# Four sixths of each layer's modulation: from matmuls in the linear attention to ACT products and POOL sums during the RWKV scan

## The chip, the cores and the metric

The kernel runs on one core of one Trainium2 chip. The metric is the device time of one execution in microseconds (us), as the median of several runs. The engines are TensorE (PE in the rows, with its weight loads as PEld), VectorE (DVE), ScalarE (ACT), GpSimd (POOL) and SyncE (SP), which here issues nearly all DMA transfers. Each engine carries out its instructions in the order in which they stand in its own list, and waits at an instruction until what it needs is there.

## What is computed

Two layers of a token mixer and a feed-forward net work on 1024 latent tokens and 256 context tokens, width 1024, in fp32. All inputs of the mixer come from one projection (`w_in`); three mixers (retention, gated linear attention, RWKV) run on their parts of it. Each layer's norms are modulated by six vectors of 1024 numbers, once for the latent tokens and once for the context:

```python
mod_l = jax.nn.silu(c) @ w_mod[l] + b_mod[l]          # w_mod[l]: 1024 x 6144
mod_c = jax.nn.silu(c_ctx) @ w_mod[l] + b_mod[l]
sh1, sc1, gt1, sh2, sc2, gt2 = jnp.split(mod_l[:, None, :], 6, axis=-1)
...
u_lat = (_modulate(_rmsnorm(x, norm_mix_pre[l]), sh1, sc1) @ w_in[l]).astype(jnp.float32)
...
x = x + gt1 * _rmsnorm(y_lat, norm_mix_post[l])
f_lat = _swiglu(_modulate(_rmsnorm(x, norm_ffn_pre[l]), sh2, sc2), w_ffn_gate[l], w_ffn_up[l], w_ffn_down[l])
x = x + gt2 * _rmsnorm(f_lat, norm_ffn_post[l])
```

The change concerns the product of the two vectors with `w_mod`. Its first two parts (`sh1`, `sc1`) are wanted at the start of a layer, the other four (parts 2 to 5) only after the mixers.

## The kernel before

A layer runs in stages. First comes the RWKV preparation, then the scan: 20 calls of `next(rw)` (index k), each one step over chunks of 64 tokens in both directions. A step is a chain of small matmuls (ra, rd, rs), ACT copies (R, BKT, Ot) and VectorE updates (Sp). Its inputs come from DRAM by SP in tiles X (one buffer), SAV and XE. The chunk matrices behind it are inverted on POOL in five blocks of four chunks (lines 731 to 736), written out and read again as XE.

Beside the scan TensorE works on *dense tiles*: the projection's columns for the linear attention (`gla_in`) and for retention (`ret_in`). One dense tile is 24 matmuls, eight slices by three products of high and low parts (whi, wlo, xh, xl), into a PSUM bank `pd`. There are three such banks, handed out in program order (`pd()`, line 198). The result goes through a tile `st` to DRAM. `gla_back` (line 1809), a part of the linear attention's backward sweep, also uses pd banks.

What the scan's 20 steps do not reach of the dense tiles follows in the tail: `rwkv_out` (transposes `pn<-ident,fo`, POOL's fo and fy), the rest of `ret_in`, and the first calls of `ret`, whose matmuls write `rr`. Then the pools of the scan are closed, and the linear attention (`gla`, matmuls into `pg`) runs in PA = 7 calls together with the rest of retention. The modulation runs there: `mods(1)` in each call takes one part from the list `todo`, which is parts 2 to 5 of this layer, and in layer 0 also parts 0 and 1 of layer 1. One part in `mod` is sixteen loads of 256 KB (`wmod`, four buffers), 32 fp32 matmuls with the two vectors as weights (2 columns) and 256 columns of `w_mod` moving (64 records in the trace), four ACT copies, two transposes and two VectorE adds.

A scheduler sets each engine's order from the program's order, priorities and its own planning of times; the `high_priority` blocks bring `rt` and `ro` forward in the tail.

Of the kernel before, what the change touches and what calls it, by code (L numbers as in the profile page):

```python
# [10 lines left out]
AF = mybir.ActivationFunctionType  # L11
ALU = mybir.AluOpType
# [5 lines left out]
KT = 8  # L18
# [59 lines left out]
def blk_of(i):  # L78
    if i < 2:
        return 0, 128 * i  # L80
    if i < 6:
        return 1, 128 * (i - 2)
    return 2, 128 * (i - 6)
# [88 lines left out]
class Kern:  # L172
# [133 lines left out]
    def mod(self, l, V, p, parts, bufs):  # L306

        nc, I = self.nc, self.I
        if l not in self.modT:
            self.modT[l] = self.t(self.G, [128, 48, 2], f"modT{l}")  # L310
        mt = self.modT[l]
        for m in parts:
            ps = self.pn()
            for kt in range(KT):
                for hf in range(2):
                    w = self.t(p, [128, 512], "wmod", bufs=bufs)
                    self.dma(w, I["w_mod"][l, 128 * kt:128 * kt + 128, 1024 * m + 512 * hf:1024 * m + 512 * hf + 512])
                    for g in range(2):
                        q = 2 * hf + g
                        self.mm(ps[32 * q:32 * q + 2, 0:256], self.sc[:, kt, :], w[:, 256 * g:256 * g + 256],  # L320
                                start=(kt == 0), stop=(kt == KT - 1))
            row = self.t(p, [128, 256], "mrow", bufs=1)
            nc.vector.memset(row, 0.0)
            for g in range(4):
                nc.scalar.copy(row[32 * g:32 * g + 2, :], ps[32 * g:32 * g + 2, 0:256])
            pt = self.pn()
            for q in range(2):
                nc.tensor.transpose(pt[:, 128 * q:128 * q + 128], row[:, 128 * q:128 * q + 128], self.ident)
            bm = V["b_mod"][:, 8 * m:8 * m + 8].rearrange("p (g q) -> p g q", q=2)
            for s in range(2):  # L330
                nc.vector.tensor_tensor(
                    mt[:, 8 * m:8 * m + 8, s].rearrange("p (g q) -> p g q", q=2),
                    pt[:, 0:256].rearrange("p (q g r) -> p g q r", g=4, r=32)[:, :, :, s], bm, op=ALU.add)

    def mod_gain(self, l, V, part_scale, gname, add_one):

# [414 lines left out]
    def gla_in(self, l, W1, xh, xl, ctx_out):  # L751
        nc, I = self.nc, self.I
        w_in = I["w_in"][l]

        def qk(t0):
            c = GLA0 + (0 if t0 < 2 else 192)
            wh, wl = self.weights(W1, [(64 * h, w_in[:, c + 48 * h:c + 48 * h + 48]) for h in range(4)], 256)
            for t in (t0, t0 + 1):
                for b in range(3):
                    if b == 0 and t < 2 and not ctx_out:  # L760
                        continue
                    n0, n = BLK[b]
                    ps = self.pd()
                    self.dense_cm(ps[:, :n], wh, wl, xh[b], xl[b], 128 * (t % 2))
                    for o in range(0, n, 256):
                        st = self.t(self.st, [128, 256], "st", bufs=6)
                        if t < 2:
                            self.act(st, ps[:, o:o + 256], AF.Copy, scale=48.0 ** -0.5)
                        else:
                            nc.scalar.copy(st, ps[:, o:o + 256])  # L770
                        self.dma(self.QK[l][:, t, n0 + o:n0 + o + 256], st)
                    yield n / 100

        def vg(m):
            wh, wl = self.weights(W1, [(0, w_in[:, GLA0 + 384 + 256 * m:GLA0 + 640 + 256 * m])], 256)
            for i in range(10):
                b, o = blk_of(i)
                if i < 2 and m == 2 and not ctx_out:
                    continue
                ps = self.pd()  # L780
                self.dense_tm(ps[:, :256], wh, wl, xh[b][:, :, o:o + 128], xl[b][:, :, o:o + 128])
                st = self.t(self.st, [128, 256], "st", bufs=6)
                v = 256 if m == 0 else (128 if m == 1 else 0)
                self.evac(st, ps[:, :256])
                if v < 256:
                    self.silu(self.st, st[:, v:], st[:, v:])
                self.dma(self.VG[l][128 * i:128 * i + 128, 256 * m:256 * m + 256], st)
                yield 2.56

        yield from qk(2)  # L790
        yield from vg(0)
        yield from vg(1)
        yield 0
        yield from qk(0)
        yield from vg(2)

    def ret_in(self, l, W1, xh, xl, ctx_out):
        nc, I = self.nc, self.I
        w_in = I["w_in"][l]
        for m in (1, 2, 0, 3):  # L800
            wh, wl = self.weights(W1, [(0, w_in[:, 256 * m:256 * m + 256])], 256)
            for i in range(10):
                b, o = blk_of(i)
                if i < 2 and m in (0, 3) and not ctx_out:
                    continue
                ps = self.pd()
                self.dense_tm(ps[:, :256], wh, wl, xh[b][:, :, o:o + 128], xl[b][:, :, o:o + 128])
                st = self.t(self.st, [128, 256], "st", bufs=6)
                self.evac(st, ps[:, :256])
                if m == 3:  # L810
                    self.silu(self.st, st, st)
                self.dma(self.UR[l][128 * i:128 * i + 128, 256 * m:256 * m + 256], st)
                yield 2.56
# [952 lines left out]
    def run(self):  # L1766
# [7 lines left out]
        f = self.f_tiles(F, range(3))  # L1774
# [12 lines left out]
        for l in range(DEPTH):  # L1787
            V = self.V[l]
            ctx_out = l < DEPTH - 1
# [6 lines left out]
            rw = self.rwkv(l, V, ctx_out)  # L1796
# [10 lines left out]
            gi = self.gla_in(l, W1, xh, xl, ctx_out)  # L1807
            ri = self.ret_in(l, W1, xh, xl, ctx_out)
            gb = self.gla_back(l, gbk)
            for k in range(20):  # L1810
                next(rw)
                if k < N1:
                    run(gi, 77 / N1)
                if k == N1 - 1:
                    for c in gi:
                        if GA and c == 0:
                            break
                if N1 <= k < N2:
                    run(chain(gi, ri), DT / (N2 - N1))
                    run(gb, GR)  # L1820
            for _ in rw:
                pass
            self.grw.__exit__(None, None, None)
            gpsr.__exit__(None, None, None)
            self.banks = (0, 0, 1)
# [2 lines left out]
            gX, X = self.pool("X", side=self.o)  # L1828
            rt = self.ret(l, ctx_out, X)
            ro = self.rwkv_out(l, V, ctx_out, pf)  # L1830
            todo = [(l, m) for m in (2, 3, 4, 5)] + ([(1, 0), (1, 1)] if ctx_out else [])

            def mods(k):
                while k and todo:
# [49 lines left out]
            f = self.f_tiles(self.F01, bs)  # L1884
# [83 lines left out]
```

## Time and profile before

| | |
|---|---|
| median of 3 runs | 4197.41 us (4195.5 to 4204.27) |
| profiled execution, its own time | 4200.48 us |
| its span, first to last instruction | 4198.7 us |
| mean granted clock of TensorE | 0.951 of full speed |
| busy in the span: TensorE, VectorE, ACT, POOL | 3837.7 (91%), 2668.9 (64%), 1740.9 (41%), 1678.4 (40%) us |

Busy times are unions of intervals by engine. Matmuls are pipelined: one that follows another at 0.12 us may have a duration of 0.28. In layer 0 the scan lies from about 366 to 755 us of the span, the tail to 896, the linear attention to 1105; in layer 1 the scan ends at about 2950, the tail at 3055 and the linear attention at 3190.

### The profile page before, as it was taken

The page shows a single profiled execution, that of the slowest core. Times are in us where ns is not written, and L with a number is a line of the kernel's source. Part 1 is how long each engine was busy: PE and PEld are TensorE (multiplying, and loading weights), DVE is VectorE, ACT ScalarE, POOL GpSimd, SP SyncE. Part 2 cuts the span into 40 slices and gives each one's busy share as a digit, 9 for nine tenths or more (in the row PEclk, how much of TensorE's full clock was granted, in tenths as well). Part 3 has the DMA queues.
Part 4 walks back from the last instruction along what each step waited for, and adds up shares of the span by engine and source line. Part 5 has one row for each costly group of instructions (what it writes and reads, how often), then busy time and mean ns, then how long its engine had stood idle before and what let it go on. Part 6 is the DMA issues. An engine that isn't in the chain of part 4 may idle for free. (4 is left out here: it accounts for less than half of the span.)

```text
span 4198.7 us, 78278 instructions
## 1 busy us (share of the span) xinstructions
PE 3837.7 (91%) x30414; PEld 3170.7 (76%) x30414; DVE 2668.9 (64%) x4510; ACT 1740.9 (41%) x3490; POOL 1678.4 (40%) x1775
## 2 busy tenths in 40 slices
PE   6998999789988899999997997999889887999998
PEld 3777887776667888887785676888856667999876
DVE  3465657667647766665765464667667578556665
ACT  4443334244435644433423443343244355344432
POOL 3146630333338832224533245740433454222453
PEclk8998999999999899999998997999989889999999
DMA  5587545666433422225331387655673132212542
GB/s 174 137 229 192 142 130 151 186 188 192 141 122 126 151 103 80 81 90 192 132 106 55 86 232 198 137 140 141 206 225 117 57 126 89 86 71 95 185 163 95
DMA packets 624771, 582.55 MB, mean 139 GB/s; under 512 B 315276, under 2 KB 517264, under 8 KB 607504
## 3 DMA queue, kind: packets, MB, share of 16 engines
q1 hardware_dynamic: 624112, 576.50, 45.0%
q8 instruction: 240, 3.93, 0.4%
q0 software_dynamic: 288, 1.05, 0.1%
q14 instruction: 131, 1.07, 0.1%
HBM read 431.14 MB, written 146.28 MB: 138 GB/s over the span
## 5 line engine op out<-in xcount | busy, mean ns | idle before, releaser
L1464 POOL TENSOR_TENSOR slo<-raw,shi 128x512 fp32r<-128x512 f32 x467 | 690.9, 1494 | 964.6 <-ACT shi L1463 894.0
L1463 ACT CAST shi<-raw 128x512 fp32r<-128x512 f32 x478 | 293.0, 619 | 492.7 <-PE pd L246 196.3
L1741 DVE TENSOR_TENSOR f<-pm,f 128x512 f32<-128x512 f32 (+1 forms) x400 | 252.1, 635 | 186.7 <-PE pm L246 184.5
L246 PE MATMUL pm<-hh,shi 128*128 128x512 f32 (+1 forms) x880 | 333.8, 380 | 19.5 <-DVE f L1741 10.2
L246 PE MATMUL pm<-hl,shi 128*128 128x512 f32 (+1 forms) x880 | 327.2, 372 | 0.0
L246 PE MATMUL pm<-hh,slo 128*128 128x512 f32 (+1 forms) x880 | 326.3, 371 | 0.0
L447 POOL TENSOR_TENSOR wlo<-wraw,whi 128x512 fp32r<-128x512 f32 x120 | 166.8, 1399 | 386.7 <-ACT whi L446 376.1
L246 PE MATMUL pd<-whi,xh 128*128 128x256 f32 x1072 | 315.6, 296 | 1.9 <-DVE st L451 1.9
L246 PE MATMUL pd<-wlo,xh 128*128 128x256 f32 x1072 | 314.5, 294 | 1.8 <-POOL wlo L447 1.8
L246 PE MATMUL pd<-whi,xl 128*128 128x256 f32 x1072 | 315.0, 294 | 0.0
L246 PE MATMUL pd<-xl,whi 128*128 128x512 f32 (+1 forms) x720 | 278.1, 387 | 12.5 <-POOL xl L390 8.6
L246 PE MATMUL pd<-xh,whi 128*128 128x512 f32 (+1 forms) x720 | 276.9, 385 | 11.6 <-DVE xh L388 11.5
L246 PE MATMUL pd<-xh,wlo 128*128 128x512 f32 (+1 forms) x720 | 271.5, 377 | 1.1 <-POOL wlo L447 1.1
L1463 ACT CAST shi<-tw 128x512 fp32r<-128x512 f32 x200 | 123.6, 619 | 305.3 <-PE pd L246 231.9
L246 PEld LDWEIGHTS pd<-wlo,xh 128*128 128x128 f32 x1072 | 211.5, 197 | 10.3 <-issue 6.0
L246 PEld LDWEIGHTS pd<-whi,xh 128*128 128x128 f32 x1072 | 210.9, 197 | 9.2 <-DVE st L451 2.5
L246 PEld LDWEIGHTS pd<-whi,xl 128*128 128x128 f32 x1072 | 211.2, 197 | 5.8 <-issue 3.7
L246 PEld LDWEIGHTS pm<-hh,shi 128*128 128x128 f32 x880 | 167.5, 191 | 58.0 <-DVE f L1741 18.3
L246 PEld LDWEIGHTS pm<-hl,shi 128*128 128x128 f32 x880 | 167.8, 191 | 29.6 <-issue 1.7
L246 PEld LDWEIGHTS pm<-hh,slo 128*128 128x128 f32 x880 | 167.2, 190 | 28.9
L1464 DVE TENSOR_TENSOR slo<-tw,shi 128x512 fp32r<-128x512 f32 x200 | 145.1, 727 | 67.0 <-ACT shi L1463 66.7
L246 PEld LDWEIGHTS pd<-xl,whi 128*128 128x128 f32 x720 | 141.5, 197 | 53.3 <-POOL xl L390 13.5
(395 smaller groups left out, 11218.4 us busy)
## 6 DMA issues: line engine op xcount, KB each, us to landing
raw<-in_wgu SPq DMA_DIRECT2D x72, 1024.0 KB
wmod<-in_w_mod SPq DMA_DIRECT2D x192, 256.0 KB
raw<-in_wd SPq DMA_DIRECT2D x44, 1024.0 KB
wraw<-in_w_in SPq DMA_DIRECT2D x100, 256.0 KB
a<-ops SPq DMA_DIRECT2D x80, 288.0 KB
h<-h SPq DMA_DIRECT2D x44, 512.0 KB
h<-u SPq DMA_DIRECT2D x19, 1024.0 KB
X<-ops SPq DMA_DIRECT2D x36, 480.0 KB
```

The source lines that it names most:

```text
L246: return self.nc.tensor.matmul(out, l, r, start=start, stop=stop, skip_group_check=skip)
L447: nc.gpsimd.tensor_tensor(wl[i][:, :, w], r, wh[i][:, :, w].bitcast(F32), op=ALU.subtract)
L1463: self.nc.scalar.copy(hi, src)
L1464: e.tensor_tensor(lo, src, hi.bitcast(F32), op=ALU.subtract)
L1741: nc.vector.tensor_tensor(facc[b][:, m, :], ps, facc[b][:, m, :], op=ALU.add)
```

## The change

`mod_wide` computes parts 2 to 5 in half parts of 512 columns. For each of the eight slices of 128 rows it loads 128x512 of `w_mod`; ACT multiplies it by the vector's number of each partition (a Copy with a scale per partition), once for each of the two vectors, and POOL adds the product to the sum `macc`. The first slice goes straight into the sum. After eight slices eight fp32 matmuls with a column of ones (weights: 128 columns of macc) add over the partitions into a pd bank, and two VectorE adds bring in the bias. The buffers are: wmod two, mprod one, macc one. The second product is written over the loaded slice. Four slices are called for behind each scan step from k = 2 on (`N1` to `N2`), the rest behind the scan's last step and ahead of the closing of its pools. The list in the linear attention keeps only parts 0 and 1 of layer 1. The buffers of `st` in `gla_in` and `ret_in` go from six to four.

```diff
+    def mod_wide(self, l, V, p, parts):
...
+        for m in parts:
+            for hf in range(2):
+                acc = self.t(p, [128, 2, 512], "macc")
+                for kt in range(KT):
+                    w = self.t(p, [128, 512], "wmod", bufs=2)
+                    c = 1024 * m + 512 * hf
+                    self.dma(w, I["w_mod"][l, 128 * kt:128 * kt + 128, c:c + 512])
+                    v = (w, self.t(p, [128, 512], "mprod")) if kt else None
+                    for s in (1, 0):
+                        self.act(acc[:, s] if kt == 0 else v[s], w, AF.Copy, scale=self.sc[:, kt, s:s + 1])
+                        if kt:
+                            nc.gpsimd.tensor_tensor(acc[:, s], acc[:, s], v[s], op=ALU.add)
+                    yield
+                ps = self.pd()
+                for s in range(2):
+                    for j in range(4):
+                        self.mm(ps[:, 4 * s + j:4 * s + j + 1], acc[:, s, 128 * j:128 * j + 128], self.ones[:, 0:1])
+                o = 8 * m + 4 * hf
+                for s in range(2):
+                    nc.vector.tensor_tensor(mt[:, o:o + 4, s], ps[:, 4 * s:4 * s + 4], V["b_mod"][:, o:o + 4], op=ALU.add)
...
-                        st = self.t(self.st, [128, 256], "st", bufs=6)
+                        st = self.t(self.st, [128, 256], "st", bufs=4)
...
+            gmw, pmw = self.pool("pmw", side=self.a)
+            mw = self.mod_wide(l, V, pmw, (2, 3, 4, 5))
             for k in range(20):
                 next(rw)
...
                 if N1 <= k < N2:
                     run(chain(gi, ri), DT / (N2 - N1))
                     run(gb, GR)
-            for _ in rw:
-                pass
+                for _ in range(4):
+                    next(mw, None)
+            for g in (rw, mw):
+                for _ in g:
+                    pass
+            gmw.__exit__(None, None, None)
...
-            todo = [(l, m) for m in (2, 3, 4, 5)] + ([(1, 0), (1, 1)] if ctx_out else [])
+            todo = [(1, 0), (1, 1)] if ctx_out else []
```

In the order of instructions the change shows at two places. The first is TensorE in the tail of layer 0: dense matmuls (whi, wlo with xh, xl into pd) and the transposes of the RWKV output (ident with fo). Before, around one of these transposes:

```order
L246 MATMUL pd_8869<-whi_1319_7998,xh_108_313 128x256
L246 MATMUL pd_8869<-wlo_1321_8000,xh_108_313 128x256
L246 MATMUL pd_8869<-whi_1319_7998,xl_109_314 128x256
L1425 MATMUL pn_9756<-ident_67,fo_9743 128x128 x3
L246 MATMUL pd_8869<-whi_1319_7998,xh_108_313 128x256
L246 MATMUL pd_8869<-wlo_1321_8000,xh_108_313 128x256
```

Now, at the sixth of the eight half parts:

```order
L246 MATMUL pd_8399<-whi_1421_8380,xl_107_312 128x256
L1452 MATMUL pn_10280<-ident_67,fo_10267 128x128 x3
L1452 MATMUL pn_10389<-ident_67,fo_10376 128x128 x3
L246 MATMUL pd_8427<-ones_69,macc_7891 128x1 x8
L246 MATMUL pd_8649<-whi_1420_8379,xh_106_311 128x256
L246 MATMUL pd_8649<-wlo_1422_8381,xh_106_311 128x256
L246 MATMUL pd_8649<-whi_1420_8379,xl_107_312 128x256
L1452 MATMUL pn_10498<-ident_67,fo_10485 128x128 x3
```

The eight matmuls on macc stand between two dense tiles, and the dense matmuls of the next tile and the next transpose come behind them.

The second place is SP in the scan of layer 0, which issues the loads of a step: XE and SAV of the scan's chunk, X of a later one, and for the linear attention glr, gk, ur. Before:

```order
L249 DMA glr_6228<-lrg_16_85 16x128 x2
L249 DMA ur_22_91<-st_5967 128x256
L249 DMA XE_8358<-af_36_105 128x6x32
L249 DMA XE_8358<-xe_46_115 128x6x96
L249 DMA gk_6232<-qk_18_87 128x2x128
L249 DMA SAV_8355<-vt_49_118 64x384 x2
```

Now:

```order
L249 DMA wmod_5586<-in_w_mod 128x512
L249 DMA wmod_5851<-in_w_mod 128x512
L249 DMA wmod_5858<-in_w_mod 128x512
L249 DMA XE_8564<-af_35_104 128x6x32
L249 DMA XE_8564<-xe_45_114 128x6x96
L249 DMA gk_6096<-qk_18_87 128x2x128
L249 DMA wmod_5865<-in_w_mod 128x512
L249 DMA ur_22_91<-st_5803 128x256
L249 DMA SAV_8561<-vt_49_118 64x384 x2
```

The loads of `w_mod`, each of which needs one of two buffers to be free, stand ahead of and between the loads of the scan step.

## Rows read from the trace of the kernel before

**Rows 1.** Stretches A:B: length, busy us (count) by engine, clock, DMA share, GB/s.
```profile
366.00:620.00 254.00, 241.12 (x3412) 211.76 (x3412) 154.49 (x340) 93.09 (x268) 140.21 (x232) 0.97 0.56 142
620.00:750.00 130.00, 124.47 (x2128) 104.93 (x2127) 90.32 (x225) 53.32 (x155) 6.71 (x12) 1.00 0.49 138
750.00:890.00 140.00, 115.78 (x998) 109.42 (x998) 78.91 (x204) 33.73 (x81) 47.11 (x52) 0.94 0.61 179
896.00:1105.00 209.00, 192.30 (x1696) 127.48 (x1690) 163.42 (x378) 95.76 (x241) 82.80 (x85) 0.97 0.63 198
...
2945.00:3055.00 110.00, 95.65 (x814) 91.18 (x816) 67.78 (x181) 24.34 (x58) 46.41 (x59) 0.95 0.70 207
3055.00:3190.00 135.00, 120.05 (x989) 76.72 (x981) 93.09 (x223) 54.52 (x140) 41.34 (x45) 0.89 0.66 209
```

The engines stand in the order PE, PEld, DVE, ACT, POOL.

**Rows 2.** Stretches, instructions that touch wmod alone: PE busy, PEld busy.
```profile
905.00:1105.00 200.00, 39.04 (x368) 8.19 (x368) 0.99 0.62 197
3050.00:3182.00 132.00, 30.38 (x256) 5.23 (x256) 0.88 0.69 217
```

**Rows 3.** TensorE's waits, 905 to 1110 us: us in total, times, longest.
```profile
PE pn L246 <- DMA wmod<-in_w_mod: 6.6, 6, 1.5
```

**Rows 4.** Groups of POOL and ACT by shape: count | busy us, mean ns | idle before.
```profile
L447 POOL TENSOR_TENSOR wlo<-wraw,whi 128x512 fp32r<-128x512 f32 x20 | 26.0, 1309 | 91.7 <-ACT whi L446 91.7
...
L372 POOL TENSOR_TENSOR nacc<-nacc,nsq 128x512 f32<-128x512 f32 x33 | 49.9, 1511 | 33.8 <-ACT nsq L239 31.6 <-PE pm L246 2.2
...
L239 ACT ACTIVATE nsq<-f 128x512 f32<-128x512 f32 x81 | 51.0, 629 | 67.8 <-DVE nacc L370 40.6 <-POOL nacc L372 15.6 <-DVE f L412 6.6
```

The first is of 366 to 760 us, the others of the whole span.

**Rows 5.** TensorE in time, retention's products: start us, us, instruction, count.
```profile
986.11 0.39 PE L246 MATMUL rr<-Sl,qx 128*128 128x64 f32 x2
986.33 0.39 PE L246 MATMUL rr<-v,sc 128*128 128x64 f32 x2
```

**Rows 6.** SP and TensorE in time: a wmod load and the matmul it releases.
```profile
970.91 0.33 SPq L249 DMA_DIRECT2D wmod<-in_w_mod  x1
...
974.50 0.60 PE L246 MATMUL pn<-wmod,silc 128*2 128x256 f32 x4 [0.60 <-DMA wmod<-in_w_mod]
```

**Rows 7.** ACT in time: the scan's copy R in steps 13, 15, 19; layer 1, 18.
```profile
653.60 0.46 ACT L1341 COPY R<-ra 128x384 f32<-128x384 f32 x1
...
688.83 0.47 ACT L1341 COPY R<-ra 128x384 f32<-128x384 f32 x1
...
749.98 0.48 ACT L1341 COPY R<-ra 128x384 f32<-128x384 f32 x1 [1.55 <-PE ra L246]
...
2926.15 0.48 ACT L1341 COPY R<-ra 128x384 f32<-128x384 f32 x1 [1.32 <-PE ra L246]
```

**Rows 8.** TensorE in time, the tail of layer 0, and layer 1's last dense matmul.
```profile
775.40 1.21 PE L246 MATMUL pd<-guout,gz 128*128 128x130 f32 x4 [9.29 <-DVE gz L1006]
...
780.96 0.41 PE L246 MATMUL pd<-whi,xl 128*128 128x256 f32 x1
781.17 0.41 PE L246 MATMUL pd<-whi,xh 128*128 128x256 f32 x1
...
889.99 0.28 PE L246 MATMUL pd<-wlo,xh 128*128 128x256 f32 x1
890.11 0.28 PE L246 MATMUL pd<-whi,xl 128*128 128x256 f32 x1
...
3054.02 0.28 PE L246 MATMUL pd<-whi,xl 128*128 128x256 f32 x1
```

**Rows 9.** POOL and SP in time: an inverse written out, the later read of its block.
```profile
390.79 1.90 POOL L736 COPY LT<-L 96x1024 f32<-96x1024 f32 x1
...
431.45 1.80 SPq L249 DMA_DIRECT2D XE<-xe  x1
```

**Rows 10.** VectorE's update Sp, groups of 400 to 500 us and of 610 to 750.
```profile
L1353 DVE TENSOR_TENSOR Sp<-SD,PC 64x384 f32<-64x384 f32 x10 | 6.7, 666 | 0.2
...
L1353 DVE TENSOR_TENSOR Sp<-SD,PC 64x384 f32<-64x384 f32 x14 | 7.7, 552 | 0.3
```

More of the change, by code (lines that the diff above doesn't have):

```diff
@@ L333, in mod @@
                     pt[:, 0:256].rearrange("p (q g r) -> p g q r", g=4, r=32)[:, :, :, s], bm, op=ALU.add)
+    def mod_wide(self, l, V, p, parts):
+        nc, I = self.nc, self.I
+        if l not in self.modT:
+            self.modT[l] = self.t(self.G, [128, 48, 2], f"modT{l}")
+        mt = self.modT[l]
+        for m in parts:
[18 more added lines that the diff above has]
+                    nc.vector.tensor_tensor(mt[:, o:o + 4, s], ps[:, 4 * s:4 * s + 4], V["b_mod"][:, o:o + 4], op=ALU.add)
     def mod_gain(self, l, V, part_scale, gname, add_one):
@@ L781, in vg @@
                 self.dense_tm(ps[:, :256], wh, wl, xh[b][:, :, o:o + 128], xl[b][:, :, o:o + 128])
-                st = self.t(self.st, [128, 256], "st", bufs=6)
+                st = self.t(self.st, [128, 256], "st", bufs=4)
                 v = 256 if m == 0 else (128 if m == 1 else 0)
@@ L807, in ret_in @@
                 self.dense_tm(ps[:, :256], wh, wl, xh[b][:, :, o:o + 128], xl[b][:, :, o:o + 128])
-                st = self.t(self.st, [128, 256], "st", bufs=6)
+                st = self.t(self.st, [128, 256], "st", bufs=4)
                 self.evac(st, ps[:, :256])
```

## The prediction

> **What bounds the kernel now.** I read first the table of busy times by stretch, because the change touches three stages of each layer and leaves the rest alone: the RWKV scan, the tail behind it (the last dense tiles, the RWKV output, the start of retention), and the linear attention. [rows 1] has them for layer 0 in order of time (scan in two stretches, tail 750 to 890, linear attention 896 to 1105) and for layer 1 the tail (2945 to 3055) and linear attention (3055 to 3190). What the reader is to see: TensorE is busy 241 of 254 and 124 of 130 us in the scan, 116 of 140 in the tail and 192 of 209 in the linear attention, so it sets the pace nearly everywhere; there it has instructions in one fixed order, and what stops one stops all behind it. VectorE is next in the linear attention (163 and 93 us). POOL is busy 140 of 254 us in the first part of the scan, 7 of 130 in the second.
>
> Then I read the wmod instructions in the linear attention [rows 2]: 39.0 us of TensorE in layer 0 (six parts of the modulation, of which two stay there) and 30.4 us in layer 1 (four parts, all moved). Last I read the order of the instructions of both kernels, since what stands behind a new wait on TensorE decides here.
>
> **Linear attention: what is removed.** Layer 0 loses four of six parts, 4/6 x 39.0 = 26.0 us of TensorE, and of the 6.6 us in which TensorE stands for wmod loads [rows 3] some 4 us. Layer 1 loses 30.4 us. TensorE's 192 us in layer 0 fall to 166, and VectorE's 163 are then as long; in layer 1 TensorE falls from 120 to 90 and VectorE's 93 is the longer. So not all is gained: I take 24 us in layer 0 and 21 in layer 1 (two thirds of 30.4, since the wall there is 135 and the next engine stands close), **-45 us**. Bounds: -30, if the two engines wait for each other by turns, and -61 for all that is removed.
>
> **One group of the new work.** Each layer's four parts become eight half parts, which I call groups: eight loads, sixteen ACT products, fourteen POOL additions, eight fp32 matmuls of one column into a bank of the dense tiles (pd), two VectorE adds. POOL: the trace has no such addition before, but two of the same size, 1.31 us (two inputs, rounded) and 1.51 us (accumulating, all fp32) [rows 4]. I take 1.3: the lines on either side differ only by what else runs. 14 x 1.3 = 18.2. ACT: 0.63 us a product, by a 128x512 activation [rows 4]. The eight matmuls have 128 weight columns in fp32 like those of retention's 64-column products, which follow each other at 0.22 us [rows 5]: 1.8 us, at worst twice that. But a group is not bound by POOL alone: wmod has two buffers, and a buffer is free only after POOL's addition. Its round is the load, 3.6 us from issue at 970.91 to the matmul it releases at 974.50 [rows 6], a product of 0.63, and two additions, 2.6: 6.8 us for two slices, so 27 us a group (G). Bounds: 21 (POOL's 18.2, a first product pair 1.3, matmuls 1.8) and 34, if each slice waits another 0.9 us behind other work in ACT's and SP's queues.
>
> The Trainium skill (GPSIMD Engine Reference, section "Performance versus the Vector engine") speaks against the change: it keeps ordinary elementwise work on VectorE, about twice as fast, and gives GpSimd some 2.6 cycles an element at 1.2 GHz for two inputs. My estimate from that is 1.11 us for 512 elements; the rows here show more, 1.31 and 1.51. By the page's price G would be about 26 instead of 27, and the sum about 10 us lower.
>
> **The gates, and where they stand.** Each group takes one pd bank in program order, and there are three banks. So in TensorE's order only two dense tiles (48 matmuls of 256 columns) stand between one group's matmuls and the next: each group is a gate, and everything behind it on TensorE waits if POOL isn't done. In layer 0 the gates stand at the 13th, 15th, 17th and 19th scan steps, and four more in the tail; in layer 1 at the 12th to 18th. macc has one buffer, so group n+1 starts on POOL only when gate n has been passed.
>
> **Scan.** Two steps take 35 us (653.6 to 688.8) and later 31 each (688.8 to 750.0 for four) [rows 7], against G = 27: groups 2 to 4 just keep pace, and the gates hold nothing long. What is added: 32 matmuls, 7 us of TensorE in a stretch in which it has 4% to spare; ACT products in order ahead of the scan's own ACT work; and wmod loads in SP's queue ahead of the scan's loads, each waiting for POOL. The 14 additions of group 1 stand among POOL's inverse of the second scan block, 18 us; there the write-out at 390.8 is followed by its reader only at 431.5 [rows 9], 40 us later, so that stays covered (without the cover some 10 us a layer). VectorE also runs slower beside a busy POOL: the Sp update takes 666 ns from 400 to 500 us, while POOL inverts, and 552 from 610 on, where POOL is nearly idle [rows 1, 10]; a tenth of a microsecond on an instruction is small. I take +8 a layer, **+16**; bounds 0 and +40.
>
> The Trainium skill (same page, section "Specifications") says that GpSimd and VectorE share SBUF interfaces, with contention for VectorE instructions with two SBUF inputs. The trace agrees in direction, with the 666 against 552 ns above; no sum rests on it.
>
> **Tail, layer 0.** Now it runs like this: scan over at about 755, a wait of 9.3 us, dense matmuls 0.21 us apart at first (780.96, 781.17) and 0.12 later (889.99, 890.11), last dense matmul at 890.1 [rows 8]. TensorE does not wait for any modulation there. After the change the fourth gate falls at about 752 (749.98 and the rest of that step), and then four groups come with nothing but 48 dense matmuls, 5.8 us, and RWKV output work between them. POOL is the slow one: gate 8 at 752 + 4 x 27 = 860. Behind gate 8 stand 600 dense matmuls and all of retention (its first state products follow 48 later), and the linear attention starts only when the dense tiles are done. 600 x 0.12 = 72, and 10 for retention's matmuls between them and for slow spacing after waits: last dense matmul at 942 instead of 890, **+52**. As a cross-check: before, by the order, 308 dense matmuls are left after the tenth transpose group, now 648; 340 x 0.12 = 41, and the wait for gate 8 on top.
>
> **Tail, layer 1.** Fourth gate at 2926.15 and some 2 us [rows 7]; gate 8 at 2928 + 108 = 3036; 504 dense matmuls behind it, 60, and 10: 3106 against 3054.0 [rows 8], **+52**. With G = 21 each layer's tail is +28, with G = 34 +80: bounds +56 and +160 for both.
>
> The buffers of st fall from six to four. They carry dense tiles' results to DRAM; a tile leaves TensorE every 24 x 0.12 = 2.9 us, four buffers give 11.6 us for a store whose like (a load, above) takes 3.6: nothing.
>
> **Sum.** 104 + 16 - 45 = +75. The profiled execution took 4200.48 us (span 4198.7), so 4275.5 for such a one; the median of the runs is 3.1 us lower: **4272**.
>
> **Rivals.** (1) *Faster: the gates fall into time that TensorE has anyway.* Place: gates 5 to 8. Then only -45 and 64 x 0.22 = 14 us of matmuls remain: 4197 - 45 + 14 = 4166. For it: POOL is idle two thirds of the tail (47 of 140 us). Against: it needs a group to be ready in about 6 us of dense work, or much of it done ahead, and one macc forbids that. It decides where G falls below about 10. Chance 0.09. (2) *No change:* G = 21, tail +56, scan nothing, and all 61 us of the linear attention are gained: 4192 to 4200. For it: TensorE is the busiest engine there. Against: VectorE at 163 of 209, and the round of two buffers. Chance 0.07. (3) *Much slower: wmod loads hold up the scan.* A load that waits for POOL stands in SP's queue ahead of the scan's XE, SAV and X loads; X has one buffer. If that costs 3 us a step in 13 steps, 40 us a layer, and G is 34, the sum is 80 + 160 - 45 = +195: 4392. For it: the order has up to three wmod loads ahead of such loads. Against: POOL is nearly idle from 620 on. Chance 0.14. My forecast, 4205 to 4345, has 0.70.
>
> The likeliest case is slower by 1.8%. A measurement of this kernel can tell about 0.2%, 8 us, from no change. Faster by more: rival 1 and the low end of rival 2, 0.10; within: 0.06; slower: 0.84. The range for 8 in 10 runs from 4200 (rival 2 left out mostly, rival 1 wholly) to 4350 (part of rival 3).
>
> **What would show it.** Right: TensorE's waits name POOL's macc, some 10 to 20 us at each of gates 5 to 8; the tail of layer 0 ends near 940, or as late after the scan as that; the linear attention of 209 and 135 us becomes about 185 and 114; wmod issues on SP wait for POOL. Wrong: no wait at the gates of the tail (rival 1); a scan longer by over 20 us a layer, with SP's waits ahead of X or XE (rival 3); a linear attention that doesn't shorten, which would mean VectorE's chain sets it and would add up to 45 us; a macc addition far from 1.3 us, which moves G, and the sum by 8 times as much.

## The result and the profile after

The changed kernel takes 4430.26 us (median of 3 runs, 4419.09 to 4432.49) against 4197.41 before: 1.0544 times as long, 95% interval 1.051 to 1.0577. It is 233 us slower, three times the 75 us that were forecast and outside the range, which ended at 4350.

Four marks of each layer cut the program into stages: the scan's first copy R on ACT, its last copy Ot, the first matmul of the linear attention (pg from wa and glr), and retention's last transpose (rr from y) at the end of that stage. Their times, from the rows of both traces, give this (us, each figure rounded by itself):

| stage | before | after | difference | forecast |
|---|---|---|---|---|
| layer 0 scan (first R to last Ot) | 371 | 433 | +63 | +8 |
| layer 0 tail (to the first pg) | 139 | 211 | +71 | +52 |
| layer 0 linear attention (to the last rr from y) | 206 | 206 | 0 | -24 |
| layer 1 scan | 356 | 420 | +64 | +8 |
| layer 1 tail | 114 | 181 | +67 | +52 |
| layer 1 linear attention | 179 | 156 | -23 | -21 |
| all the rest of the span | 2832 | 2820 | -12 | 0 |

How far such stages differ by themselves can be read from the run st4 below, whose time is that of before: its stages differ from those of before by up to 7 us, the rest of the span by 15. A difference of that size, here and in the tables below, says nothing.

Table of busy times of the changed kernel by stage, columns as in [rows 1]: the scan of layer 0 in two stretches, its tail and linear attention, then layer 1's tail and linear attention.

```profile
381.00:655.00 274.00, 256.76 (x3532) 226.37 (x3530) 179.15 (x351) 105.00 (x285) 148.79 (x234) 0.94 0.52 134
655.00:814.00 159.00, 142.44 (x2018) 121.45 (x2016) 92.88 (x208) 83.10 (x190) 65.77 (x58) 0.80 0.49 142
814.00:1025.00 211.00, 141.50 (x1032) 131.66 (x1032) 87.99 (x221) 70.58 (x140) 110.65 (x106) 0.77 0.55 157
1025.00:1232.00 207.00, 181.76 (x1488) 135.45 (x1488) 166.17 (x377) 89.62 (x229) 82.33 (x86) 0.90 0.39 120
3135.00:3317.00 182.00, 120.66 (x883) 112.68 (x880) 82.69 (x211) 58.44 (x113) 101.42 (x103) 0.75 0.54 158
3317.00:3473.00 156.00, 139.84 (x1080) 106.39 (x1080) 120.18 (x277) 69.07 (x176) 60.59 (x60) 0.87 0.30 90
```

What to see beside [rows 1]: the second part of the scan and the tail have a granted clock of 0.80 and 0.77 where it was 1.00 and 0.94, and in the tail POOL's work has grown from 47 to 111 us.

TensorE in time in the changed kernel: the second gate in the scan of layer 0, and the four gates of its tail (start, duration, instruction, count; idle time before it).

```profile
709.26 2.02 PE L246 MATMUL pd<-ones,macc 128*128 128x1 f32 x16
...
832.72 3.57 PE L246 MATMUL pd<-ones,macc 128*128 128x1 f32 x16 [1.38 <-POOL macc L352]
...
873.09 3.57 PE L246 MATMUL pd<-ones,macc 128*128 128x1 f32 x16 [5.98 <-POOL macc L352]
...
906.09 3.57 PE L246 MATMUL pd<-ones,macc 128*128 128x1 f32 x16 [0.33 <-POOL macc L352]
...
934.27 3.57 PE L246 MATMUL pd<-ones,macc 128*128 128x1 f32 x16 [17.50 <-POOL macc L352]
```

The fourth gate stands at 798, so groups 5 to 8 took 34, 40, 33 and 28 us. Waits of TensorE and SP in the whole of the changed kernel, and of ACT and SP in the later part of layer 1's scan (2965 to 3130 us): us in total, times, longest.

```profile
PE pd L246 <- POOL macc L352: 52.8, 7, 17.5
```

```profile
SPq L249 <- POOL macc L352: 145.2, 80, 5.9
```

```profile
ACT mprod L239 <- DMA wmod<-in_w_mod: 23.4, 14, 3.6
...
SPq L249 <- POOL macc L352: 37.4, 21, 5.3
```

TensorE waits for POOL only in the tail. In the scan it never does; there ACT waits for the new loads, and SP for POOL.

### The profile page after: what moved, and what is told of

Its sections match the earlier page's. It is cut to its first block, busy times and chain, and to the rows that moved or that the text cites. A ratio compares the mean times of both kernels' runs of the same rounds, so it can differ in the third digit from the quotient of the medians.

```text
span 4428.4 us, 78451 instructions
## 1 busy us (share of the span) xinstructions
PE 3923.0 (89%) x30142; PEld 3278.9 (74%) x30142; DVE 2732.9 (62%) x4518; ACT 1902.4 (43%) x3714; POOL 1967.2 (44%) x1999
## 3 DMA queue, kind: packets, MB, share of 16 engines
q14 instruction: 135, 1.11, 0.1%
## 5 line engine op out<-in xcount | busy, mean ns | idle before, releaser
L246 PE MATMUL pd<-whi,xh 128*128 128x256 f32 x1072 | 328.3, 308 | 0.0
L246 PE MATMUL pd<-wlo,xh 128*128 128x256 f32 x1072 | 326.2, 305 | 1.4 <-POOL wlo L474 1.4
L246 PE MATMUL pd<-whi,xl 128*128 128x256 f32 x1072 | 324.7, 304 | 0.0
L352 POOL TENSOR_TENSOR macc<-macc,mprod 128x512 f32<-128x512 f32 x112 | 146.2, 1305 | 218.6 <-ACT macc L239 119.7
L246 PEld LDWEIGHTS pd<-wlo,xh 128*128 128x128 f32 x1072 | 223.1, 208 | 11.9 <-issue 7.8
L246 PEld LDWEIGHTS pd<-whi,xh 128*128 128x128 f32 x1072 | 223.0, 209 | 6.4 <-issue 3.4
L246 PEld LDWEIGHTS pd<-whi,xl 128*128 128x128 f32 x1072 | 223.1, 208 | 5.3 <-issue 3.5
```

What stands on the lines that cost most here:

```text
L246: return self.nc.tensor.matmul(out, l, r, start=start, stop=stop, skip_group_check=skip)
L352: nc.gpsimd.tensor_tensor(acc[:, s], acc[:, s], v[s], op=ALU.add)
```

## The experiments

Fourteen kernels were run, in four sets; each set has its own runs of the kernel before (4198 to 4203 us), and the differences below are against those. "The column sums" are the eight matmuls of each group, "gates" their places in TensorE's order.

### First set: the matmuls or what feeds them

**cols_only**: macc is cleared once, the gates stay.

```diff
-                acc = self.t(p, [128, 2, 512], "macc")
...
                 for kt in range(KT):
-                    w = self.t(p, [128, 512], "wmod", bufs=2)
...
-                            nc.gpsimd.tensor_tensor(acc[:, s], acc[:, s], v[s], op=ALU.add)
                     yield
```

> The changed kernel without its loads of w_mod, ACT products and POOL sums: macc is set to zero once, and the eight matmul groups on macc stand in TensorE's order where they stood (parts 2 to 5 of the modulation are left out). Theory A, the one-column matmuls halve the granted clock for some 10 us behind each group: the clock from 655 on in the scan of layer 0 stays near 0.8 to 0.85, the scan stays about 30 us a layer longer than before, time 4230 to 4270. Theory B, what feeds the groups (loads in SP's queue, products in ACT's queue) makes the scan late and the idle time lowers the clock: clock 1.00 and a scan as before, time 4165 to 4185.

4234.4 us, +31. The time fits theory A, the mechanism doesn't: the clock is 0.97 from 620 to 755, with two short dips, one behind a gate and one behind an idle stretch. The scan is 12 us (layer 0) and 27 us (layer 1) longer than before, the tail 11 and 18.

**no_cols**: loads, products and sums without the column sums.

```diff
-                ps = self.pd()
-                for s in range(2):
-                    for j in range(4):
-                        self.mm(ps[:, 4 * s + j:4 * s + j + 1], acc[:, s, 128 * j:128 * j + 128], self.ones[:, 0:1])
...
-                    nc.vector.tensor_tensor(mt[:, o:o + 4, s], ps[:, 4 * s:4 * s + 4], V["b_mod"][:, o:o + 4], op=ALU.add)
+                    nc.vector.tensor_tensor(mt[:, o:o + 4, s], acc[:, s, 0:4], V["b_mod"][:, o:o + 4], op=ALU.add)
```

> The changed kernel with loads, products and sums, but without the 128 column-sum matmuls (VectorE adds the bias to four columns of macc, so parts 2 to 5 are not the reference's). Theory A: the clock in the scan returns to 0.95 or more, the scan is at most 25 us a layer longer than before, time 4190 to 4240. Theory B: the scan stays 50 us or more a layer longer, though no group stands on TensorE, time 4270 or more. In both the tail of layer 0 (scan's end to the linear attention's first pg) shrinks from over 200 us to about 145, since nothing on TensorE waits for POOL there.

4373.25, +170: theory B's side. The tail of layer 0 falls to 119 us, but the scan is longer than in the changed kernel, 479 us from first to last copy R (420 there, 364 before): without gates nothing holds the groups back, and all eight run in the scan. VectorE's costliest instructions in the scan of layer 0, first before, then here (count | busy us, mean ns):

```profile
L648 DVE TENSOR_TENSOR SR<-rd,rwmask 64x192 f32<-64x192 f32 x152 | 52.6, 354 | 5.7 <-PE rd L246 3.0
L1353 DVE TENSOR_TENSOR Sp<-SD,PC 64x384 f32<-64x384 f32 x36 | 21.7, 603 | 0.8
...
L1266 DVE TENSOR_TENSOR BK<-X 128x192 f32<-128x192 f32 x35 | 18.0, 513 | 0.0
L1265 DVE TENSOR_TENSOR BK<-X 128x192 f32<-128x192 f32 x34 | 14.7, 432 | 25.6 <-PE rd L1322 17.1 <-ACT X L239 8.4
```

```profile
L671 DVE TENSOR_TENSOR SR<-rd,rwmask 64x192 f32<-64x192 f32 x152 | 52.6, 354 | 11.1 <-PE rd L246 8.5
L1288 DVE TENSOR_TENSOR BK<-X 128x192 f32<-128x192 f32 x36 | 41.5, 1152 | 32.5 <-PE rd L1345 14.6 <-ACT X L239 7.5 <-DMA xe<-L 5.1
L1289 DVE TENSOR_TENSOR BK<-X 128x192 f32<-128x192 f32 x36 | 39.3, 1091 | 0.0
L1376 DVE TENSOR_TENSOR Sp<-SD,PC 64x384 f32<-64x384 f32 x36 | 37.8, 1050 | 0.7
```

The instructions with both operands in SBUF take up to 2.7 times as long; SR, which reads one operand from PSUM (rd), takes 354 ns in both.

**cols64**: 64 columns moving in place of one.

```diff
-                        self.mm(ps[:, 4 * s + j:4 * s + j + 1], acc[:, s, 128 * j:128 * j + 128], self.ones[:, 0:1])
+                        self.mm(ps[:, 256 * s + 64 * j:256 * s + 64 * j + 64], acc[:, s, 128 * j:128 * j + 128], self.ones[:, 0:64])
```

> The changed kernel, its 128 column-sum matmuls with 64 equal columns of ones moving in place of one (each sum is computed 64 times, one is read). Theory A, it is the lack of columns that lowers the clock: the clock behind the groups stays at 1.00 in the scan, and the time falls by 40 to 80 us, to about 4370. Theory B, or a lowered clock that doesn't come from the columns: 4430, or 4440 with the added columns.

4406.9, +204 against +233 of the changed kernel; the intervals of the two ratios (1.0416 to 1.0567, 1.051 to 1.0577) overlap, so the gain is unclear. The clock is another matter. TensorE in stretches of 4 us around the gate at 709 in the changed kernel and the one at 712 here (busy, clock, DMA share, GB/s):

```profile
708.00:712.00 4.00, 4.00 (x70) 0.87 0.52 116
712.00:716.00 4.00, 4.00 (x37) 0.50 0.98 343
716.00:720.00 4.00, 4.00 (x18) 0.50 0.33 119
720.00:724.00 4.00, 4.00 (x49) 0.85 0.49 108
```

```profile
712.00:716.00 4.00, 4.00 (x62) 1.00 0.80 232
716.00:720.00 4.00, 4.00 (x54) 1.00 0.53 187
720.00:724.00 4.00, 3.99 (x71) 1.00 0.74 179
```

Behind the one-column group the clock stands at its lower level for some 8 us though TensorE is busy throughout; with 64 columns it doesn't fall there, only behind idle stretches elsewhere; from 655 to 809 it is 0.86 on the mean, against 0.80 in the changed kernel from 655 to 814. In cols_only most gates leave it at 1.00 too, so the one column is not enough by itself; what else it takes was not settled. By the times of cols64 and cols_only it is a small part of the 233 us.

**no_mod**: the kernel before without parts 2 to 5.

```diff
-            todo = [(l, m) for m in (2, 3, 4, 5)] + ([(1, 0), (1, 1)] if ctx_out else [])
+            for s in range(2):
+                self.nc.vector.tensor_copy(self.modT[l][:, 16:48, s], V["b_mod"][:, 16:48])
+            todo = [(1, 0), (1, 1)] if ctx_out else []
```

> The kernel before without parts 2 to 5 of the modulation (the bias alone is taken for them), so the gain in the linear attention alone. My forecast took 45 us for both layers: 4152. The changed kernel's linear attention gave about 5 us in layer 0 and 25 in layer 1: if that is all there is to gain, 4167; if the linear attention of layer 0 gains 20 us or more here, then the changed kernel lost it to something else (the lower clock there, 0.90 against 0.97).

4180.01, -23 (ratio 0.9929 to 0.9956), less than in either expectation. The linear attention goes from 206.4 to 205.6 us in layer 0 and from 179.5 to 165.7 in layer 1. Its stretches here, layer 0 and 1:

```profile
898.00:1104.00 206.00, 181.82 (x1487) 133.57 (x1486) 168.06 (x377) 90.44 (x228) 83.15 (x86) 0.91 0.39 121
3049.00:3214.00 165.00, 144.60 (x1030) 111.31 (x1030) 115.68 (x264) 68.31 (x174) 57.99 (x60) 0.81 0.29 86
```

In layer 0 TensorE's busy time falls by 10 us, not 26, and the granted clock from 0.97 to 0.91. TensorE's waits change too: those that name VectorE there add up to 3 us before and to 16 here (15 in the changed kernel). So the whole prize of the change, if the new work cost nothing at all, was 23 us.

### Second set: the feed taken apart, without column sums

These start from no_cols (+170). **nc_noload** makes all products from one resident slice (two product buffers), **nc_nosum** drops the additions, **nc_noprod** the products, **half** cuts each addition into four of 128 columns.

```diff
-                    self.dma(w, I["w_mod"][l, 128 * kt:128 * kt + 128, c:c + 512])
...
+                    w = self.w0[1]
```

```diff
-                            nc.gpsimd.tensor_tensor(acc[:, s], acc[:, s], v[s], op=ALU.add)
```

```diff
-                        self.act(acc[:, s] if kt == 0 else v[s], w, AF.Copy, scale=self.sc[:, kt, s:s + 1])
...
+                            nc.gpsimd.tensor_tensor(acc[:, s], acc[:, s], w, op=ALU.add)
```

```diff
+                            for h in range(4):
+                                nc.gpsimd.tensor_tensor(acc[:, s, 128 * h:128 * h + 128], acc[:, s, 128 * h:128 * h + 128],
+                                                        v[s][:, 128 * h:128 * h + 128], op=ALU.add)
```

> The kernel without column sums (no_cols, 4373 us, its scan 479 us in layer 0 against 364 before), and without its loads of w_mod: one slice is loaded once a layer, all products are made from it, into two buffers. All ACT products and POOL sums stay; parts 2 to 5 are left out of the result. Theory S, loads that wait in SP's queue hold up the scan's loads: the scan falls to 365 to 390 us, the time to 4180 to 4230. Theory P, POOL's additions slow VectorE's instructions, which are on the scan's chain: the scan stays at 450 us or more, time 4330 or more.

> no_cols without its POOL additions: loads and ACT products stay (the products are not added up). Theory P: the scan of layer 0 falls to 365 to 390 us and VectorE's Sp update and BK products to their durations of before (552 and 440 ns), time 4180 to 4230. Theory S falls too here, as a buffer no longer waits for POOL; theory Q, the products themselves hold up ACT's queue while they wait for loads: the scan stays over 430 us, time over 4310.

> no_cols without the ACT products behind the first slice: POOL adds the loaded slice itself, twice; loads and additions stay. Theory Q: the scan of layer 0 falls to 365 to 390 us. Theories P and S: it stays at 450 us or more, time 4330 or more.

> no_cols with each POOL addition of 512 columns cut into four of 128. Theory P, with the wait as long as the POOL instruction that VectorE meets: VectorE's BK products (953 ns on the mean in the second part of the scan, 440 before) and Sp update (729, 552 before) lose most of what they were longer by, and the time falls by 40 us or more, to 4330 or below, although POOL has more instructions. If VectorE only shares a rate with POOL, or under theories S and Q: no less than 4373, and more if the four together take longer than one.

| | difference | first to last R, layer 0, 1 | Sp, BK products, ns (scan of layer 0, from 386 on) |
|---|---|---|---|
| before | 0 | 364, 350 | 603, 432 and 513 |
| no_cols | +170 | 479, 480 | 1050, 1152 and 1091 |
| nc_nosum | +17 | 400, 373 | 587, 405 and 446 |
| nc_noload | +213 | 497, 511 | 1211, 1005 and 758 |
| nc_noprod | +234 | 513, 524 | 1124, 709 and 666 |
| half | +273 | 566, 528 | 1027, 479 and 641 |

Theory P is right here: only without POOL's additions does the scan come back, and then not wholly. 36 and 23 us remain, with VectorE's instructions as short as before, and layer 0's 400 us lie above the 365 to 390 that were expected. Without loads or products the additions come faster, and it gets worse. A second way in which POOL hurts shows there: single steps of 60 to 95 us (81 to 105 in `half`), as POOL's additions stand among its inverses. The copies with which POOL writes an inverse out, in layer 1, of the kernel before (first R at 2591), the changed one (2715) and nc_noload (2697):

```profile
2600.02 1.99 POOL L736 COPY LT<-L 96x1024 f32<-96x1024 f32 x1
2651.48 2.05 POOL L736 COPY LT<-L 96x1024 f32<-96x1024 f32 x1
```

```profile
2740.31 1.91 POOL L763 COPY LT<-L 96x1024 f32<-96x1024 f32 x1
2810.50 1.99 POOL L763 COPY LT<-L 96x1024 f32<-96x1024 f32 x1
```

```profile
2920.39 2.15 POOL L762 COPY LT<-L 96x1024 f32<-96x1024 f32 x1
```

Counted from the first R the first two come at 9 and 60 us before and at 25 and 95 in the changed kernel; the one shown of nc_noload, its second, comes at 224, within a step of 95 us (copy R at 2853, the next at 2949). `half` does not decide what it was made for: four short additions take 1.9 us where one took 1.3, the BK products recover for the most part, Sp doesn't, and the late inverses cover the rest.

### Third set: the additions with the gates in place, and the place of the work

**after_nosum**, the changed kernel without additions; **dve_sum**, with `nc.vector` for `nc.gpsimd` in that line; **late**, without the call of the groups in the scan; **st4**, the kernel before with four st buffers.

```diff
-                for _ in range(4):
-                    next(mw, None)
```

```diff
-                        st = self.t(self.st, [128, 256], "st", bufs=6)
+                        st = self.t(self.st, [128, 256], "st", bufs=4)
```

> The changed kernel without its POOL additions: loads, ACT products and the column sums stay, so parts 2 to 5 are not the reference's. If the three costs add up (without parts 2 to 5 4180; loads and products 38; additions 155; column sums 54 to 57), 4272 to 4275, with VectorE's Sp update in the scan back from 820 to about 600 ns. If the additions matter only for the groups that run in the scan, and the tail's loss comes from loads and matmuls, 4330 or more.

> The changed kernel with its 224 additions on VectorE in place of POOL (the reference's result). VectorE takes 0.64 us for such an addition (page of before), 71 us a layer. If what an addition on POOL costs the scan is the time for which it keeps VectorE from two-input work, and VectorE's chain sets the end, VectorE pays 0.64 us in place of up to 1.3: 4340 to 4400. If VectorE only runs a little slower beside POOL, then 71 us of work of its own in the chain cost more than that: 4460 or more.

> The changed kernel with nothing of the new work called for during the scan: all eight groups of a layer come behind it. The scan is as before (364 and 350 us between the first and last copy R, against 420 and 411). If a group takes 27 us there, as I had it, gate 8 falls 216 us behind the scan's end, the tail grows by some 170 us a layer, and the time is about 4500; if the groups are quicker without the scan beside them (20 us, POOL's own time), about 4400.

> The kernel before with four st buffers in place of six, and nothing else: the one part of the change that stands apart. The same as before within 0.3%, 4190 to 4212. Over 4215 would mean that a part of the loss is the dense tiles waiting for their stores.

after_nosum: 4339.3, +140. The number is that of the second expectation, 4330 or more, but the stages are the other way round: the scan stays as long as in the changed kernel (433 and 413 us against 433 and 420), and the tail falls from 211 to 155 and from 181 to 151. With the gates in place POOL's additions cost the tail, and the scan's loss comes from something else. (In layer 0 two differences cancel: without the additions the scan's first twelve steps are 18 us shorter and its last seven 18 us longer; the second was not explained.) dve_sum: 4384.0, +185, in the range of the first alternative; VectorE's Sp update is back from 820 to 609 ns, though each addition takes VectorE 0.75 us. But the reason given there isn't shown by it: the scan gains only 7 and 9 us, the tail 22 and 9. late: 4595.4, +396. Its gates in the tail:

```profile
890.84 3.57 PE L246 MATMUL pd<-ones,macc 128*128 128x1 f32 x16 [22.95 <-POOL macc L352]
917.74 3.57 PE L246 MATMUL pd<-ones,macc 128*128 128x1 f32 x16 [23.33 <-POOL macc L352]
945.92 3.57 PE L246 MATMUL pd<-ones,macc 128*128 128x1 f32 x16 [24.61 <-POOL macc L352]
...
999.41 3.57 PE L246 MATMUL pd<-ones,macc 128*128 128x1 f32 x16 [23.29 <-POOL macc L352]
1026.24 3.58 PE L246 MATMUL pd<-ones,macc 128*128 128x1 f32 x16 [23.25 <-POOL macc L352]
```

A group takes 26.8 us where it has POOL to itself (the G of 27), and TensorE stands for 23 of them. The total was missed upwards, 4595 for 4500: the first gate stands 59 us behind the end of layer 0's scan (775 to 834), so gate 8 ends at 1030, and the scans were still 21 and 17 us longer, nearly all of it in their first twelve steps, where group 1 runs on POOL all the same. st4: 4193.9, ratio 0.9965 to 1.0005: nothing, as forecast.

### Fourth set: loads or products, with the column sums

**g_prod** is after_nosum without its loads (one resident slice), **g_load** after_nosum without its products.

```diff
-                    self.dma(w, I["w_mod"][l, 128 * kt:128 * kt + 128, c:c + 512])
...
+                    w = self.w0[1]
```

```diff
-                        self.act(acc[:, s] if kt == 0 else v[s], w, AF.Copy, scale=self.sc[:, kt, s:s + 1])
+                        if kt == 0:
+                            self.act(acc[:, s], w, AF.Copy, scale=self.sc[:, kt, s:s + 1])
```

> Column sums and ACT products, no loads of w_mod behind the first slice of a layer and no POOL additions (products from one resident slice; parts 2 to 5 are not the reference's). In after_nosum, with the loads, the last seven steps of the scan take 165 and 155 us (115 and 110 before, 122 and 136 with the column sums alone). Theory R, a ring of ACT and SP: a product waits on ACT for its load, the load stands on SP behind a store that waits for ACT: without loads the last seven steps fall to 120 to 140 us in both layers, time 4240 to 4270. Theory Q2, the 0.7 us of a product in front of the scan's own copies: they stay at 150 or more, time 4310 or more.

> Column sums and the loads of w_mod, no ACT products behind the first slice and no POOL additions. Theory R: no product waits on ACT, so the last seven steps of the scan take as long as with the column sums alone, 120 to 140 us, time 4235 to 4260. Theory S, loads ahead of the scan's own loads in SP's queue: 150 or more, time 4310 or more.

g_prod: 4224.1, +26, its last seven steps 127 and 123 us: in the total, products alone cost nothing. In layer 0 the stages do move: the scan is 31 us longer than in cols_only, most of it in its first twelve steps, and the tail 22 shorter, with 936 TensorE records in it instead of 1050, so a part is dense work that now runs earlier. g_load: 4304.1, +106, last seven steps 140 and 146. So loads alone cost much, less than loads and products together (165 and 155): theory S for the larger part, theory R for the rest. Waits of SP, ACT and TensorE in g_load, 2900 to 3050 us, and of ACT in after_nosum, 655 to 810:

```profile
SPq L249 <- DMA wmod<-in_w_mod: 50.9, 23, 4.2
...
ACT P L239 <- DMA X<-ops: 38.2, 8, 13.8
...
PE pd L246 <- ACT gkhT L1058: 21.9, 3, 10.4
```

```profile
ACT mprod L239 <- DMA wmod<-in_w_mod: 46.2, 22, 5.0
```

In g_load nobody reads the slices, so a load waits only for the one before it in its buffer; SP stands 51 of 150 us. In the last seven steps it issues a load of X up to 10 us after the last reader of its buffer (before: at most 1.1 us). ACT then stands for X up to 13.8 us, the linear attention's copy gkhT stands behind that in ACT's order, and TensorE waits for gkhT up to 10.4 us. With products ACT stands for the loads as well, ahead of the scan's copies, and its wait for X isn't longer than before. ACT's wait for X in the last seven steps of layer 1, before and in the changed kernel:

```profile
ACT P L239 <- DMA X<-ops: 27.2, 6, 5.8
```

```profile
ACT P L239 <- DMA X<-ops: 14.2, 10, 2.9
```

No kernel gave the loads a queue of their own or more buffers, so the order in SP's queue is read from the waits and not tested by itself. Against a lack of DMA bandwidth speaks the DMA engines' mean busy share in these steps, 0.52 in g_load and 0.48 before.

## Why the prediction was wrong

With the gates in place, the kernels make a ladder, each with one part more (differences against before): no_mod -23, cols_only +31, g_load +106, after_nosum +140, the changed kernel +233. So the column sums cost 54 us, the loads 75, the products that wait for them 34, POOL's additions 93. The 95% intervals of the rungs reach 6 to 17 us to either side, so the 34 is the least sure; and the ladder has one order only, in another the parts could share the time otherwise. What each does in which stage, from one trace of each (us, the difference from the rung below; the first column is cols_only against before):

| stage | column sums | loads | products | additions |
|---|---|---|---|---|
| scan, layer 0 and 1 | +12, +27 | +32, +16 | +19, +14 | 0, +7 |
| tail, layer 0 and 1 | +11, +18 | +8, +3 | -3, +16 | +56, +30 |

**The scan, forecast +16, measured +127, is the step that failed.** Its parts were named, but priced in a lump of 8 us a layer instead of one by one. The 7 us a layer of TensorE for the matmuls were 12 and 27: they go into a stage in which TensorE has 4% to spare, in the middle of its chain, and in layer 1 the clock of the last seven steps was 0.87 in cols_only. The loads in SP's queue (48) and the products behind them (33) belong to rival 3's mechanism. In g_load the place is the one that it named, X with its one buffer; in the changed kernel ACT stands for the new loads instead (23.4 us from 2965 to 3130), and not longer for X than before. Rival 3 had 40 us a layer for it and the low chance of 0.14, against which I put that POOL is nearly idle from 620 on. That was the wrong counter-argument: the loads wait for their buffers, and SP's and ACT's queues are in order, whoever is idle; without POOL's additions the scan is as long within 7 us. Rival 3 had the right kind of time, 4392, and still fell short.

**The clock had no term.** The sum took every TensorE instruction of the scan at its length of before. TensorE in the last seven steps of the scan (from the 13th copy R to the 20th), layer 0 and 1, before and in the changed kernel (columns as in [rows 1]):

```profile
634.50:750.00 115.50, 109.97 (x1914) 92.06 (x1913) 81.14 (x205) 47.41 (x140) 5.25 (x11) 1.00 0.50 140
...
2830.90:2940.80 109.90, 106.33 (x1891) 88.90 (x1892) 79.01 (x203) 45.09 (x135) 1.39 (x7) 1.00 0.48 136
```

```profile
654.30:801.10 146.80, 132.61 (x1916) 113.03 (x1916) 88.95 (x201) 75.71 (x176) 58.52 (x50) 0.79 0.50 146
...
2964.70:3126.30 161.60, 137.87 (x1930) 116.01 (x1930) 94.63 (x209) 88.63 (x197) 74.16 (x63) 0.81 0.50 143
```

About as many records, now with column sums among them, take 133 and 138 us in place of 110 and 106, and the idle time grows only from 6 to 14 and from 4 to 24. So of the 83 us that these steps grow by, some 54 are TensorE's own work taking longer at a lower granted clock, and 29 are waits. No kernel held the clock, so what the waits alone would have cost is not shown.

**"So that stays covered"**, the cover of group 1's additions in the inverses, held in part only. The inverses come 25 and 45 us later in layer 0, 16 and 35 in layer 1, and the first twelve steps grow by 24 and 10 us (late, which runs group 1 there and none of the others in the scan, shows 21 and 13). In after_nosum, with the inverses in time, they grow by 6 and 9: so the late inverses go with 18 us in layer 0, and in layer 1 the cover held.

**The tail, forecast +104, measured +139**, had the right mechanism: gates 5 to 8 stand in it, TensorE waits there for POOL's macc, and with the additions taken away 86 us of it go. The size of G was right (26.8 in late, 27 forecast; an addition 1.30 and 1.34 us, 1.3 forecast); in the tail itself it was 28 to 40, as POOL also has the RWKV output's work there. The bound I had was 34, and one group went past it. What stands behind gate 8 was right: from the end of its matmuls (937.8) to the last dense matmul (1019.7) 82 us, 82 forecast. The waits were not as forecast, 10 to 20 us at each gate: only gate 8 had one, 17.5 and 15.8 us, the others 0 to 6.6. TensorE came late to them, as it also waited for the RWKV output (fy and fo, 22 us in layer 0, 6 before, under 2 in after_nosum) and had a clock of 0.77 and 0.75.

**The linear attention, forecast -45, measured -24**: right in layer 1 (-23 for -21; no_mod, with the same work removed, gained 14 there), wrong in layer 0 (0 for -24). The step "TensorE's 192 us fall to 166" is what failed: they fell to 182, with the granted clock at 0.90 instead of 0.97. no_mod shows the same (0.91) without any of the new work. The bound -30 for engines that wait for each other by turns was the nearest to it, and still too high a gain. TensorE's waits for VectorE, 3 us before and 15 and 16 here, speak for that bound, and for the sign named in the prediction, that VectorE's chain sets the stage; whether these waits or the clock hold its length is open.

**Right**: the sign, who is waited for in TensorE's and SP's waits (POOL's macc), and that the st buffers do nothing. **The range** was too narrow upwards: it counted the bounds of G, but no bound above 40 us for both scans, though nothing in the trace of before showed a queue with such loads in it.

On the additions the Trainium skill can be weighed in two places. GPSIMD Engine Reference, "Specifications", has contention on shared SBUF interfaces with VectorE instructions that have two SBUF inputs: the trace of no_cols agrees closely, Sp and the BK products growing from 603, 432 and 513 to 1050, 1152 and 1091 ns and SR, with one operand in PSUM, staying at 354. I had looked at 666 against 552 ns and called it small; that was beside POOL instructions most of which were half as long, 0.64 to 0.79 us from 400 to 500. In the changed kernel itself Sp takes 820 ns, and the scan is as long without the additions, so there it cost nothing that shows. The Trainium skill's section "Performance versus the Vector engine" would have put the additions on VectorE, about twice as fast: the run agrees in direction (dve_sum 4384 against 4430; 0.75 us against 1.32 for an addition). The price by the 2.6 cycles an element that the Trainium skill gives there, 1.11 us by my estimate, was lower than what was measured.

No version that does the whole work is faster than the kernel before. no_mod leaves all the work out and gains 23 us, so any way to do it elsewhere has that much to spend, and the column sums alone cost 54.

## What to carry to other kernels

Before moving work off the busiest engine, ask what taking it away alone gives: here 23 of the 56 us that TensorE spent on it, as in layer 0 TensorE came to wait for VectorE and its clock was 0.91 in place of 0.97. Then price the move per queue: a load with few buffers in an in-order queue costs every load behind it its wait, and a product that waits for the load costs again on its own engine, however idle the engine behind both may be. Give waits of the busiest engine more than their length: here its own work behind them took longer, at a lower clock. And a small matmul that takes a bank from a rotation becomes a gate for everything that uses the same rotation behind it.

## What the runs showed of the hardware that I had not expected

In the changed kernel TensorE is at the lower granted clock for about 8 us behind eight one-column matmuls, although its row says busy (0.50 from 712 to 720); with 64 columns it stayed at 1.00, and so it mostly did with one column where nothing fed the groups. It is so too behind a stretch in which TensorE stands (the changed kernel: length, TensorE's busy time, clock, DMA share, GB/s):

```profile
728.00:732.00 4.00, 1.25 (x32) 0.93 0.59 164
732.00:736.00 4.00, 3.87 (x33) 0.50 0.76 261
```

At the lower clock dense matmuls follow each other at 0.21 us, at the full one at 0.12 (starts at 717.02 and 717.23, and at 722.75 and 722.87). Beside a stream of POOL additions a VectorE product of 128x192 from two SBUF tiles takes 1.1 us on the mean instead of 0.5. And fewer instructions on TensorE need not shorten its busy time by their own: without four parts of the modulation it fell by 10 us instead of 26, the clock from 0.97 to 0.91.
